# First conditioning split into two column halves, and the gate rows' transposes moved behind the second head's first blocks

## The chip, the cores and the metric

The kernel runs on one core of a Trainium2 chip. The metric is the device time of one execution in microseconds (us), the median of the runs shown. The engines are TensorE (PE in the profile; its weight loads are PEld), VectorE (DVE), ScalarE (ACT), GpSimd (POOL) and SyncE (SP), which issues nearly all DMAs.

## The reference, cut to what matters

The kernel is one inference step of a two-layer encoder on 1024 prompt tokens and 32 sample tokens, D = 1024, all in float32. Layer 0 is an mLSTM mixer with four heads. What concerns the change is the conditioning of its input and the value, gate and query/key projections of it:

```python
def ada_mod(c, w, b):
    return jax.nn.silu(c) @ w + b
...
sh1, sc1, g1, sh2, sc2, g2 = jnp.split(ada_mod(c, p['w_ada'][l], p['b_ada'][l])[:, None, :], 6, axis=-1)
u = x * (1 + sc1) + sh1
...
proj = u @ w_in
qk_pre = proj[..., :2 * QK_A]
v = proj[..., 2 * QK_A:2 * QK_A + V_A]
o_pre = proj[..., 2 * QK_A + V_A:2 * QK_A + 2 * V_A]
gates = (proj[..., 2 * QK_A + 2 * V_A:] + b_if).astype(jnp.float32)
qk, conv_new = causal_conv(qk_pre, conv_prev, conv_w, conv_b)
```

There is one vector c for the prompt and one for the sample. Before any u exists, sh1 and sc1 are needed: the first 2048 columns of a 1024 x 6144 weight, 8 MiB, that meet two vectors only.

## The kernel before

Tokens lie in three blocks, `TBS`: 384, 384 and 288 (256 prompt and the 32 sample tokens). Features lie on the partitions, in `KC` = 8 chunks of 128. Products run as three float32r matmuls each (high x high, high x low, low x high).

**The first conditioning.** `ada_load(k)` (L193) loads rows 128k to 128k + 127 of the first 2048 columns as two DMAs of 512 KB, each of 1024 columns, into a buffer of the ring tag "wc", which has six. `ada_mm(k)` (L424) multiplies them by the silu of c, one matmul of 512 columns for each of the four column groups of PE, and adds up over k in one PSUM bank. `ada_first` (L430) copies that to SBUF, transposes it and adds the bias: sh1 and sc1 for all eight chunks.

**The value stage.** `x_transpose` (L403) turns a block's rows of x into columns, chunk by chunk, on PE, and copies them out. `u_chunks` (L414) makes u of a chunk: high part on ACT (L370), the unrounded value and the low part on DVE (L372, L375). `v_weight` (L465) loads one half of the rows of head 0's value weights, to which the eight gate columns are added; `split` casts it on ACT (L89) and subtracts on DVE (L90). `v_first` (L504) runs over blocks and, in a block, over chunks outside and tiles of 128 tokens inside, three matmuls each (L479 to L481), so that a chunk can be used as soon as it is made. Behind each chunk it calls `next_u` (L759), which moves the next block's transposes and u along by one chunk.

**The gate rows.** `gate_rows` (L518) transposes the gate columns (L532), then makes the log-sigmoid, its running sums and maxima as rows of four partitions, on ACT and DVE, into a tile `stk`. After `yield GATE` comes its second part: nine transposes of `stk` (L567) and two copies into `ae`, which `mlstm` reads for its weights W (L654).

**The order.** The text is traced in order, and a scheduler places each instruction by its time model, with earlier text ahead where several could run; each engine then works through its own list in order. Side work stands in generators of a `Flow`: `tick` counts a waiting time down and runs the next piece. `qk_proj` (L571) makes a head's query and key: six blocks of 24 matmuls, the convolution on DVE (L596, L599) and the silu (L451 to L454, L604, L605); behind the first two blocks of each half and behind its end it calls `after`, which ticks. `GATE` = 3.0 lets the second part of `gate_rows` be traced at the third tick, in the middle of head 0's `qk_proj`; `flow.finish(gates)` behind it runs what is left. The scores of head 0 (`S`, L656) are the first work of `mlstm`, traced behind the third unit of head 1's `qk_proj`.

Of the kernel before, what the change touches and what calls it, by code (L numbers as in the profile page):

```python
# [8 lines left out]
F32 = mybir.dt.float32  # L9
F32R = mybir.dt.float32r  # L10
AF = mybir.ActivationFunctionType
ALU = mybir.AluOpType
# [63 lines left out]
def trunk_kernel(ctx: ExitStack, tc: tile.TileContext, a, o):  # L76
# [113 lines left out]
    def wc_tile(shape, name):  # L190
        return ring.tile(shape, F32, tag="wc", name=name, bufs=6)

    def ada_load(k):  # L193

        raw = wc_tile([P, 2 * D], f"rada_0_{k}")
        for i in range(2):
            nc.sync.dma_start(raw[:, i * D:(i + 1) * D], a["w_ada"][0, k * P:(k + 1) * P, i * D:(i + 1) * D])
        return raw
# [5 lines left out]
    nc.sync.dma_start(rows2[96:112], a["b_ada_kv"].rearrange("(k p) -> k p", p=P))  # L204
    adaw = [ada_load(k) for k in range(4)]
    tp = tpt("tp_c")
# [185 lines left out]
    def rc_tile(shape, name):  # L392
        return A.tile(shape, F32, tag="rc", name=name, bufs=1)
# [29 lines left out]

    def ada_mm(k):  # L424

        for q in range(4):
            nc.tensor.matmul(ada_ps[32 * q:32 * q + 32, :512], cs[:, k, :], adaw[k][:, q * 512:(q + 1) * 512],
                             start=(k == 0), stop=(k == KC - 1))

    def ada_first():  # L430

        sb = rc_tile([P, 512], "sada")
        ps2 = nmt("adat")
        for hf in range(2):
            (nc.scalar.copy if hf else nc.vector.tensor_copy)(sb[:, 256 * hf:256 * hf + 256],
                                                              ada_ps[:, 256 * hf:256 * hf + 256])
            for b in (2 * hf, 2 * hf + 1):
                nc.tensor.transpose(ps2[:, b * P:(b + 1) * P], sb[:, b * P:(b + 1) * P], ident)
        nc.vector.tensor_tensor(
            ada[:, 0:16, :].rearrange("p (q b) j -> p q b j", q=4),  # L440
            ps2.rearrange("p (b q j) -> p q b j", b=4, q=4)[:, :, :, 0:2],
            pt2[:, 0:16].rearrange("p (q b) -> p q b", q=4)[:, :, :, None].broadcast_to([P, 4, 4, 2]), op=ALU.add)


    GATE = 3.0
    ADA_C = (2.0, 0.0, 2.0)
# [292 lines left out]
    x_load(*TBS[0])  # L739
    adaw += [ada_load(k) for k in (4, 5)]  # L740
    for k in range(4):
        ada_mm(k)
    vw = [v_weight(0, 0)]
    adaw += [ada_load(k) for k in (6, 7)]
    for k in range(4, 6):
        ada_mm(k)
    for _ in xT[0]:
        pass
    for k in range(6, 8):
        ada_mm(k)  # L750
    vw.append(v_weight(0, 1))
    x_load(*TBS[1], wc_tile)
    x_load(*TBS[2])
    ada_first()
    for _ in uT[0]:
        pass
    flow.add(small_params(), SP)

    def next_u(bi, k):  # L759
        if bi < 2:  # L760
            next(xT[bi + 1])
            next(uT[bi + 1])
            if k == KC - 1:
                for g in (xT[bi + 1], uT[bi + 1]):
                    for _ in g:
                        pass
        flow.tick()
# [17 lines left out]
    qk = [qk_proj(0, tick)]  # L785
    flow.finish(gates)
    G = A.tile([P, KC, T], F32, tag="G", name="G")
    ml = None
    for h in range(1, NH):
        unit = [0]  # L790

        def after_qk():
            unit[0] += 1
            if h > 1 or unit[0] >= 3:
                flow.tick()
        if h == 1:
            ml = flow.add(mlstm(0, *qk[0], vts[0]))
        qk.append(qk_proj(h, after_qk))
        vts.append(v_proj(h, tick))
        flow.finish(ml)  # L800
        ml = flow.add(mlstm(h, *qk[h], vts[h]))
# [1289 lines left out]
```

## Time and profile before

| | us |
|---|---|
| median of 3 runs (lowest to highest) | 2438.1 (2436.41 to 2440.5) |
| profiled execution | 2437.59 |
| its span, first to last instruction | 2435.8 |
| PE busy in the span | 2363.6 (97%) |
| DVE busy | 1987.5 (82%) |
| ACT busy | 1178.8 (48%) |

The profile gives, for each engine, the time in which it worked, and for a wait the instruction that ended it. Times in a row are us from the span's start, then the duration; "x8" counts instructions, and what stands in brackets is the idle time ahead and who ended it. A PE that is busy is not always at its peak, since matmuls overlap.

### The profile page before, as it was taken

The numbers are of one execution on the slowest core, as the hardware profiler recorded it, in microseconds if no ns is written. First come the engines' busy times: TensorE is split into PE (matmuls) and PEld (weight loads), VectorE is DVE, ScalarE is ACT, GpSimd is POOL, SyncE is SP. The second block draws the span as 40 slices with busy tenths as digits, with TensorE's granted clock in tenths as the row PEclk, the third lists the DMA queues.
The fourth block names the chain that finished last, engine by engine and source line by source line (L and its number), as shares of the span: only waits on it lengthen the run. The fifth ranks groups of instructions, "written<-read, shape, count | busy, mean of one in ns | idle before, by whom it ended". The sixth has DMA issues, their size and how long they took to land.

```text
span 2435.8 us, 44452 instructions
## 1 busy us (share of the span) xinstructions
PE 2363.6 (97%) x17180; PEld 2265.8 (93%) x17180; DVE 1987.5 (82%) x4222; ACT 1178.8 (48%) x2394; POOL 166.6 (7%) x315
## 2 busy tenths in 40 slices
PE   7999999999999999999999999999999999899997
PEld 4999999999999999999989977889999999899997
DVE  4899898788788789999697666755998888887778
ACT  4644456278566620010157566763776777222212
POOL 0211100000000000000001134420000000000003
PEclk9999999999999999999999999999999999999999
DMA  8433223436556897656423220051486779966642
GB/s 297 128 103 98 82 86 102 158 113 215 182 186 194 296 343 266 234 203 232 143 64 97 74 64 1 11 133 36 162 279 233 252 255 341 367 242 232 229 151 72
DMA packets 292151, 423.61 MB, mean 174 GB/s; under 512 B 15576, under 2 KB 221804, under 8 KB 286820
## 3 DMA queue, kind: packets, MB, share of 16 engines
q1 hardware_dynamic: 287908, 390.50, 48.3%
q10 hardware_dynamic: 4032, 30.28, 3.1%
q8 instruction: 135, 2.21, 0.4%
q14 instruction: 76, 0.62, 0.1%
HBM read 304.91 MB, written 118.17 MB: 174 GB/s over the span
## 4 chain that ended last, share of the span: by engine, by line
PE 47%; DVE 12%; DMA 5%; ACT 4%; issue 2%; POOL 1%; SPq 0%; DVEq 0%; ACTq 0%; POOLq 0%
PE dn L1415 11%; PE up L1280 9%; PE dn L120 5%; PE dn L119 5%; PE dn L118 5%; PE pv L1853 3%; PE s L1796 2%; PE pt L1831 2%; DMA rdn_u<-in_w_up_dram 1%; DVE wf_u L90 1%; PE op_b L118 1%; PE op_b L119 1%; PE op_b L120 1%; DVE HL L90 1%; DMA radw<-in_w_ada_dram 1%
## 5 line engine op out<-in xcount | busy, mean ns | idle before, releaser
L1045 DVE SCALAR_TENSOR_TENSOR ACX<-dn,ada,ACX 128x264 f32<-128x264 f32 (+6 forms) x664 | 281.9, 448 | 86.4 <-PE dn L1415 41.4
L1415 PE MATMUL dn<-fx,wf_d 128*128 128x264 f32 x2016 | 254.0, 285 | 6.5 <-DVE ACX L1045 3.5
L1415 PEld LDWEIGHTS dn<-fx,wf_d 128*128 128x128 f32 x2016 | 248.7, 188 | 8.7 <-issue 2.5
L89 ACT CAST w_dn<-raw_dn 128x1024 fp32r<-128x1024 f32 x36 | 37.7, 1050 | 284.1 <-DVE aw L274 172.8
L118 PE MATMUL dn<-hs,w_dn 128*128 128x384 f32 (+2 forms) x512 | 161.3, 316 | 0.8 <-DVE ACX L1045 0.7
L119 PE MATMUL dn<-hs,w_dn 128*128 128x384 f32 (+2 forms) x512 | 160.9, 315 | 0.0
L120 PE MATMUL dn<-hs,w_dn 128*128 128x384 f32 (+2 forms) x512 | 155.9, 314 | 1.8 <-DVE w_dn L90 1.8
L1280 PE MATMUL up<-TF,wf_u 128*128 128x264 f32 x1056 | 143.6, 285 | 1.8 <-ACT H L1283 1.8
L1280 PE MATMUL up<-u,wf_u 128*128 128x264 f32 x1056 | 139.7, 285 | 1.7 <-DVE H L1286 0.8
L1280 PE MATMUL up<-U,wf_u 128*128 128x264 f32 x1056 | 139.6, 285 | 1.6 <-DVE H L1286 1.0
L274 DVE SCALAR_TENSOR_TENSOR aw<-radw,cs,aw 128x512 f32<-128x512 f32 x196 | 139.5, 745 | 0.0
L1280 PEld LDWEIGHTS up<-TF,wf_u 128*128 128x128 f32 x1056 | 134.3, 188 | 3.1 <-ACT H L1283 3.0
L1280 PEld LDWEIGHTS up<-U,wf_u 128*128 128x128 f32 x1056 | 133.1, 188 | 2.7 <-DVE H L1286 1.9
L1280 PEld LDWEIGHTS up<-u,wf_u 128*128 128x128 f32 x1056 | 132.6, 188 | 2.7 <-ACT wf_u L89 0.8
L119 PE MATMUL dn<-U,w_dn 128*128 128x384 f32 (+2 forms) x416 | 129.8, 313 | 0.0
L118 PE MATMUL dn<-U,w_dn 128*128 128x384 f32 (+2 forms) x416 | 129.3, 311 | 0.0
L120 PE MATMUL dn<-U,w_dn 128*128 128x384 f32 (+2 forms) x416 | 125.6, 312 | 0.9 <-DVE w_dn L90 0.9
L238 DVE SCALAR_TENSOR_TENSOR ada_room<-ada_room,cs 128x256 f32<-128x256 f32 x224 | 98.9, 476 | 4.2 <-DMA ada_room<-in_w_ada_dram 4.2
L120 PEld LDWEIGHTS dn<-hs,w_dn 128*128 128x128 f32 x512 | 95.8, 188 | 2.9 <-DVE w_dn L90 2.6
L118 PEld LDWEIGHTS dn<-hs,w_dn 128*128 128x128 f32 x512 | 96.4, 188 | 1.5 <-DVE ACX L1045 1.0
L119 PEld LDWEIGHTS dn<-hs,w_dn 128*128 128x128 f32 x512 | 96.5, 188 | 0.0
L1806 DVE CUSTOM_DVE_ANT_0 p<-s,bias 128x576 f32<-128x576 f32 (+9 forms) x132 | 79.1, 606 | 20.3 <-PE s L1796 13.4
(394 smaller groups left out, 7171.5 us busy)
## 6 DMA issues: line engine op xcount, KB each, us to landing
hpl<-HL SPq DMA_DIRECT2D x144, 264.0 KB
rdn_u<-in_w_up_dram SPq DMA_DIRECT2D x64, 512.0 KB
hd<-HL SPq DMA_DIRECT2D x28, 1056.0 KB
fx<-hd SPq DMA_DIRECT2D x50, 528.0 KB
radw<-in_w_ada_dram SPq DMA_DIRECT2D x24, 1024.0 KB
hd<-HM SPq DMA_DIRECT2D x28, 792.0 KB
raw_up<-in_w_up_dram SPq DMA_DIRECT2D x40, 512.0 KB
raw_dn<-in_w_down_dram SPq DMA_DIRECT2D x36, 512.0 KB
```

The source lines that it names most:

```text
L90: (eng or nc.vector).tensor_sub(dst_l, src, dst_h.bitcast(F32))
L118: nc.tensor.matmul(ps, wh, mov(0, k), start=(k == 0), stop=False)
L119: nc.tensor.matmul(ps, wh, mov(1, k), start=False, stop=False)
L120: nc.tensor.matmul(ps, wl, mov(0, k), start=False, stop=(k == nk - 1))
L238: nc.vector.scalar_tensor_tensor(acc[:, cnd], raw[:, k], sc, acc[:, cnd], op0=ALU.mult, op1=ALU.add)
L274: nc.vector.scalar_tensor_tensor(acc[cnd], raw[:, k], sc, acc[cnd], op0=ALU.mult, op1=ALU.add)
L1045: nc.vector.scalar_tensor_tensor(xs, ps[:, off + o:off + o + mm_], gate[:, fc, cnd:cnd + 1], xs, op0=ALU.mult, op1=ALU.add)
L1280: nc.tensor.matmul(p, self.ws[w][:, wl, k], moving(f, tp, xl, k), start=first and k + n_ == 0, stop=k == 3 and n_ == 2, skip_group_check=n ...
L1415: nc.tensor.matmul(p, ws[w][:, wl, k], t[:, s0, xl], start=first and k + n_ == 0, stop=k == kg - 1 and n_ == 2, skip_group_check=not first)
L1796: nc.tensor.matmul(s[:, b, :w], qst, kk[i][:, g, k0 + j0:k0 + j0 + w], start=(i == 0), stop=(i == 1))
L1806: nc.vector.tensor_tensor_reduce(out=z.rearrange("p (b w) -> p b w", b=np_), in0=s[:, :np_, :w], in1=bt.rearrange("p (b w) -> p b w", b=np ...
L1853: nc.tensor.matmul(pv[64 * e:64 * e + 64, :nq], V[:kp, vt0 + j, g * 64:(g + 1) * 64], pts[e][:kp, j, :nq], start=(j == 0), stop=(j == nt - 1))
```

## The change

The first conditioning is loaded and multiplied by halves. Half `hf` holds 512 of the 1024 columns of sh1 and the same 512 of sc1: all that four of the eight chunks need. Half 0 is loaded first, ahead of block 0's rows; half 1 behind the first value weights. `ada_first(0)` is traced ahead of the x transposes, the first four chunks of u of block 0 follow, and `v_first` starts on them; behind its fourth chunk come half 1's products, `ada_first(1)`, block 0's last four chunks of u, and the small parameters. Block 1's transposes and u move along by two chunks for each of the last four chunks instead of by one for each of eight. `GATE` becomes 99.0, so that no tick reaches the second part of `gate_rows`, and `flow.finish(gates)` moves into head 1's `qk_proj`, behind its second block; the tile `G` is taken there too.

```diff
--- before.py
+++ after.py
@@ -190,11 +190,13 @@
     def wc_tile(shape, name):
         return ring.tile(shape, F32, tag="wc", name=name, bufs=6)
 
-    def ada_load(k):
-
-        raw = wc_tile([P, 2 * D], f"rada_0_{k}")
+    def ada_load(hf, j):
+
+        raw = wc_tile([P, 2, 2, 512], f"rada_0_{hf}_{j}")
         for i in range(2):
-            nc.sync.dma_start(raw[:, i * D:(i + 1) * D], a["w_ada"][0, k * P:(k + 1) * P, i * D:(i + 1) * D])
+            k = 2 * j + i
+            nc.sync.dma_start(raw[:, i], a["w_ada"][0, k * P:(k + 1) * P, :2 * D].rearrange(
+                "p (r h c) -> p h r c", r=2, h=2)[:, hf])
         return raw
     c_rows = raw_tile([16, P], "c_rows")
     nc.sync.dma_start(c_rows[0:8], a["c_prompt"].rearrange("b (k p) -> (b k) p", p=P))
@@ -202,7 +204,7 @@
     rows2 = raw_tile([NPT2, P], "rows2")
     nc.sync.dma_start(rows2[0:96], a["b_ada"].rearrange("l (k p) -> (l k) p", p=P))
     nc.sync.dma_start(rows2[96:112], a["b_ada_kv"].rearrange("(k p) -> k p", p=P))
-    adaw = [ada_load(k) for k in range(4)]
+    adaw = [[ada_load(0, j) for j in range(4)]]
     tp = tpt("tp_c")
     nc.tensor.transpose(tp[:, :16], c_rows, ident[:16, :16])
     cx = cp.tile([P, 4, 16], F32, name="cx")
@@ -421,28 +423,30 @@
 
     ada_ps = adat("ada_0")
 
-    def ada_mm(k):
+    def ada_mm(hf, k):
 
         for q in range(4):
-            nc.tensor.matmul(ada_ps[32 * q:32 * q + 32, :512], cs[:, k, :], adaw[k][:, q * 512:(q + 1) * 512],
+            nc.tensor.matmul(ada_ps[32 * q:32 * q + 32, 256 * hf:256 * hf + 256], cs[:, k, :],
+                             adaw[hf][k // 2][:, k % 2, q // 2, q % 2 * 256:q % 2 * 256 + 256],
                              start=(k == 0), stop=(k == KC - 1))
 
-    def ada_first():
-
-        sb = rc_tile([P, 512], "sada")
-        ps2 = nmt("adat")
-        for hf in range(2):
-            (nc.scalar.copy if hf else nc.vector.tensor_copy)(sb[:, 256 * hf:256 * hf + 256],
-                                                              ada_ps[:, 256 * hf:256 * hf + 256])
-            for b in (2 * hf, 2 * hf + 1):
-                nc.tensor.transpose(ps2[:, b * P:(b + 1) * P], sb[:, b * P:(b + 1) * P], ident)
-        nc.vector.tensor_tensor(
-            ada[:, 0:16, :].rearrange("p (q b) j -> p q b j", q=4),
-            ps2.rearrange("p (b q j) -> p q b j", b=4, q=4)[:, :, :, 0:2],
-            pt2[:, 0:16].rearrange("p (q b) -> p q b", q=4)[:, :, :, None].broadcast_to([P, 4, 4, 2]), op=ALU.add)
-
-
-    GATE = 3.0
+    def ada_first(hf):
+
+        sb = rc_tile([P, 256], f"sada{hf}") if hf else y_tile([P, 256], "sada0")
+        ps2 = nmt(f"adat{hf}")
+        for b in range(2):
+            cols = slice(b * P, (b + 1) * P)
+            (nc.scalar.copy if b else nc.vector.tensor_copy)(sb[:, cols], ada_ps[:, 256 * hf + b * P:256 * hf + b * P + P])
+            nc.tensor.transpose(ps2[:, cols], sb[:, cols], ident)
+        for r in range(2):
+            c0 = r * KC + 4 * hf
+            nc.vector.tensor_tensor(
+                ada[:, c0:c0 + 4, :].rearrange("p (q b) j -> p q b j", q=2),
+                ps2[:, :256].rearrange("p (b r q j) -> p r q b j", b=2, r=2, q=2)[:, r, :, :, 0:2],
+                pt2[:, c0:c0 + 4].rearrange("p (q b) -> p q b", q=2)[:, :, :, None].broadcast_to([P, 2, 2, 2]), op=ALU.add)
+
+
+    GATE = 99.0
     ADA_C = (2.0, 0.0, 2.0)
     w_in = a["w_in_a"][0]
 
@@ -737,33 +741,40 @@
     xT = [x_transpose(t0, n, (nc.scalar.copy, nc.vector.tensor_copy)[:2 - (i > 0)]) for i, (t0, n) in enumerate(TBS)]
     uT = [u_chunks(t0, n) for t0, n in TBS]
     x_load(*TBS[0])
-    adaw += [ada_load(k) for k in (4, 5)]
-    for k in range(4):
-        ada_mm(k)
+    for k in range(KC):
+        ada_mm(0, k)
     vw = [v_weight(0, 0)]
-    adaw += [ada_load(k) for k in (6, 7)]
-    for k in range(4, 6):
-        ada_mm(k)
+    adaw.append([ada_load(1, j) for j in range(4)])
+    ada_first(0)
     for _ in xT[0]:
         pass
-    for k in range(6, 8):
-        ada_mm(k)
     vw.append(v_weight(0, 1))
     x_load(*TBS[1], wc_tile)
     x_load(*TBS[2])
-    ada_first()
-    for _ in uT[0]:
-        pass
-    flow.add(small_params(), SP)
+    for k in range(4):
+        next(uT[0])
 
     def next_u(bi, k):
-        if bi < 2:
-            next(xT[bi + 1])
-            next(uT[bi + 1])
-            if k == KC - 1:
-                for g in (xT[bi + 1], uT[bi + 1]):
-                    for _ in g:
-                        pass
+        if bi == 0:
+            if k == 3:
+                for i in range(KC):
+                    ada_mm(1, i)
+                ada_first(1)
+                for _ in uT[0]:
+                    pass
+                flow.add(small_params(), SP)
+            if k < 4:
+                return
+            for _ in range(2):
+                next(xT[1])
+                next(uT[1])
+        elif bi == 1:
+            next(xT[2])
+            next(uT[2])
+        if bi < 2 and k == KC - 1:
+            for g in (xT[bi + 1], uT[bi + 1]):
+                for _ in g:
+                    pass
         flow.tick()
     vts = [v_first(vw, next_u)]
     for t0, n in TBS:
@@ -783,14 +794,16 @@
         ada_fix(0, [(2, "g"), (4, "sc"), (5, "g")])
     flow.add(ada_l0())
     qk = [qk_proj(0, tick)]
-    flow.finish(gates)
-    G = A.tile([P, KC, T], F32, tag="G", name="G")
     ml = None
     for h in range(1, NH):
         unit = [0]
 
         def after_qk():
+            nonlocal G
             unit[0] += 1
+            if h == 1 and unit[0] == 2:
+                flow.finish(gates)
+                G = A.tile([P, KC, T], F32, tag="G", name="G")
             if h > 1 or unit[0] >= 3:
                 flow.tick()
         if h == 1:
```

## The prediction

> **What bounds the kernel now.** I read the page first, then the stretches of the first 200 us, because all edits lie there.
>
> ```profile
> span 2435.8 us, 44452 instructions
> ...
> PE 2363.6 (97%) x17180; PEld 2265.8 (93%) x17180; DVE 1987.5 (82%) x4222; ACT 1178.8 (48%) x2394; POOL 166.6 (7%) x315
> ```
>
> TensorE (PE) is busy 97% of the span. The 72.2 us in which it is not are therefore the place to look for a gain, and time taken out of PE's own stream ahead of a full stretch should shift everything behind it. In the stretches the columns are: length, busy us and instructions of PE, of its weight loads (PEld), DVE, ACT and POOL, then the granted clock, the DMA share and GB/s.
>
> ```profile
> 16.60:20.20 3.60, 1.45 (x7) 0.74 (x8) 0.56 (x1) 0.48 (x1) 0.00 (x0) 1.00 1.03 421
> 20.20:25.00 4.80, 4.80 (x20) 1.98 (x20) 1.12 (x3) 0.96 (x2) 0.00 (x0) 0.64 1.04 385
> ...
> 29.00:34.00 5.00, 4.21 (x16) 0.58 (x16) 1.26 (x1) 0.04 (x1) 0.00 (x0) 1.00 1.03 411
> 34.00:36.45 2.45, 1.06 (x7) 0.62 (x7) 1.44 (x5) 1.13 (x3) 0.00 (x0) 1.00 1.03 410
> 36.45:70.80 34.35, 34.35 (x265) 32.15 (x266) 26.51 (x78) 25.80 (x57) 1.33 (x7) 1.00 0.73 224
> 70.80:92.70 21.90, 21.85 (x134) 21.19 (x131) 19.62 (x32) 10.93 (x18) 1.90 (x2) 1.00 0.49 142
> 92.70:94.90 2.20, 0.02 (x1) 0.00 (x0) 2.20 (x5) 1.38 (x2) 0.06 (x2) 1.00 0.04 8
> 94.90:99.60 4.70, 4.65 (x28) 4.60 (x29) 4.61 (x8) 2.86 (x4) 0.77 (x2) 0.64 0.09 33
> 99.60:140.00 40.40, 40.36 (x270) 39.34 (x270) 39.62 (x89) 29.91 (x80) 11.29 (x22) 1.00 0.20 64
> 140.00:200.00 60.00, 58.15 (x381) 53.37 (x380) 55.49 (x184) 26.53 (x80) 8.02 (x24) 1.00 0.35 104
> ```
>
> Three stages show. Until 36.45 us the DMA engines are the bound: their share is 1.03 and PE does conditioning products as rows land. From 36.45 to 70.80, the value work of the first head, PE is busy without a gap and DVE has 7.8 us to spare. At 92.70 PE stops for 2.20 us and then runs 4.70 us at a granted clock of 0.64. From there to 140 us DVE (39.62 of 40.40) is as full as PE. Who waits for whom, PE's weight loads, 36 to 140 us:
>
> ```profile
> PEld ae_ps L567 <- ACT stk L560: 2.5, 1, 2.5
> ...
> PEld S L656 <- DVE y L605: 0.4, 1, 0.4
> ```
>
> So the stop is the wait of the gate rows' transposes (L567). The second row matters as much: head 0's first score product S(0) already arrives 0.4 us too early for DVE.
>
> **Part 1: conditioning by halves.** The rows of the opening, in order of time:
>
> ```profile
> 26.03 1.07 PE L427 MATMUL ada<-rada,cs 128*32 128x512 f32 x8
> ...
> 27.97 1.07 ACT L89 CAST w_v<-raw_v 128x1056 fp32r<-128x1056 f32 x1 [0.65 <-DMA raw_v<-in_w_in_a_dram]
> 29.07 1.26 DVE L90 TENSOR_TENSOR w_v<-raw_v,w_v 128x1056 fp32r<-128x1056 f32 x1 [0.47 <-ACT w_v L89]
> ...
> 32.94 1.05 PE L427 MATMUL ada<-rada,cs 128*32 128x512 f32 x4 [0.23 <-DMA rada<-in_w_ada_dram]
> ...
> 34.04 0.42 DVE L435 COPY sada<-ada 128x256 f32<-128x256 f32 x1 [3.71 <-PE ada L427]
> 34.50 0.37 ACT L435 COPY sada<-ada 128x256 f32<-128x256 f32 x1 [5.46 <-DVE sada L435]
> ...
> 36.45 0.39 PE L479 MATMUL v<-w_v,U 128*128 128x264 f32 x1 [0.86 <-ACT U L370]
> ```
>
> Before, the last conditioning rows land at 32.94 us and the first value product starts at 36.45. After, half 0 is 4.2 MB of the 8.4, so chunks 0 to 3 need 4.2 MB plus block 0's rows (1.6 MB) and the first value weights (0.5 MB) instead of 11.0 MB. At the 400 GB/s of the window below that is 4.7 MB, 11.8 us, fewer: the data is there near 21 us. Cast and subtraction of the weights (1.07 + 1.26) put the first products near 24 us, and their 36 matmuls end before 30 us, under the cover of half 1's transfer.
>
> Chunk 4 needs all 11.0 MB still: either half 1 or the second value weights come last, in an order that I can't tell. If half 1 is last, it lands at 32.94 plus what shorter rows cost. A row of a half is 2 KB where it was 4 KB. Two windows with only such rows, 1124 to 1126 us (2 KB, radw) and 7 to 15 us (nearly all 4 KB):
>
> ```profile
> DMA packets 389, 0.80 MB, mean 398 GB/s; under 512 B 0, under 2 KB 0, under 8 KB 389
> ```
> ```profile
> DMA packets 880, 3.20 MB, mean 400 GB/s; under 512 B 99, under 2 KB 99, under 8 KB 880
> ```
>
> 398 against 400 GB/s is 0.1 us on 8.4 MB, so half 1 lands near 33.1 us. The Trainium skill's "DMA: Bandwidth & Descriptors", "Why small descriptors are slow (HBM only)", speaks against the change here: about 3 cycles of overhead a packet beside one per 32 bytes. By it two 2 KB packets take 134 cycles for the 131 of one of 4 KB, and an estimate from that page is 0.5 us on the opening instead of 0.1. The trace's two windows agree with a small loss and not with a large one.
>
> From the last landing to chunk 4: before, 36.45 - 32.94 = 3.51 us. The last product is half as wide (0.5 us less than 1.05), the two copies half as wide (about 0.1 less each), two transposes fewer (0.2), one small DVE add more (0.15, an estimate from the copies): 2.8 us, so 35.9. If the weights are last, 33.1 + 1.07 + 1.26 and two handovers give 35.6. I take 36.0: 0.45 us before the old start. Bounds: 35.6, and 36.8 if the steps run at a low clock.
>
> What is gained beside that is the work of chunks 0 to 3. In the stretch from 36.45 to 70.80 PE's stream is the bound, as these two rows show (a stretch of value products alone, and the x transposes of the whole stage):
>
> ```profile
> 64.00:70.00 6.00, 6.00 (x52) 6.00 (x51) 2.36 (x2) 1.65 (x2) 1.04 (x3) 1.00 1.03 304
> ```
> ```profile
> L410 PE MATMUL xps<-ident,xr 128*128 128x128 f32 (+1 forms) x46 | 8.3, 271 | 0.0
> ```
>
> A product comes each 6.00 / 50 = 0.12 us (two of the 52 are cut by the edges). 9 tiles x 8 chunks x 3 = 216 products make 25.9 us and the transposes 8.3: 34.2 of 34.35. Block 0's first four chunks are 3 x 4 x 3 = 36 products, 4.3 us, that now run in the wait. The stage ends 4.3 + 0.45 = 4.75 us earlier. The rest of it stays covered: DVE and ACT have 7.8 and 8.5 us to spare there and also lose four chunks of it; block 1's rows come behind the same 11.0 MB; its buffers come free as half 1's products run, as before.
>
> Against this stands PE's clock. Between the first half's end and chunk 4 PE does one product per 1.3 us. All four column groups of 512 took 1.07 us together (26.03), so 256 take 0.54: busy 41%. The nearest row, 16.60 to 20.20, is busy 1.45 / 3.60 = 40%, and behind it the clock is 0.64 for 4.80 us, 1.7 us lost; but a product at half clock is busy 0.8 of the time, like 29.00 to 34.00 (0.84, clock 1.00), so the clock may be back before chunk 4. Cost 0 to 1.7 us; I take 0.4, nearer to that last row. Part 1 in sum: 4.75 - 0.4 = 4.35 us gained, bounds 2.3 and 5.2. The small parameters move behind half 1's products, in SP's queue too; the first reader is the gate rows' bias, behind 70.80 us, so I cost that at nothing. Were they late, the gate chain would be, on the same DVE path as below.
>
> **Part 2: the gate rows' transposes.** The rows are of the gate chain's start, its end, and of S(0):
>
> ```profile
> 70.80 1.03 PE L532 MATMUL gt<-ident,g 128*36 128x128 f32 x8
> ...
> 92.42 0.30 PE L120 MATMUL qk<-U,w_qk 128*128 128x288 f32 x1
> ...
> 93.81 1.08 ACT L560 ACTIVATE stk<-tt 4x1056 f32<-4x1056 f32 x1 [0.37 <-DVE tt L559]
> ...
> 94.95 0.72 PE L567 MATMUL ae_ps<-ident,stk 36*128 36x36 f32 x9 [2.23 <-ACT stk L560]
> ```
> ```profile
> 113.56 0.95 DVE L605 SCALAR_TENSOR_TENSOR y<-y,sl 128x353 f32<-128x353 f32 x2
> ...
> 114.13 0.30 PEld L656 LDWEIGHTS S<-y,y 128*128 128x128 f32 x2 [0.36 <-DVE y L605]
> ```
>
> Stop 94.95 - 92.42 - 0.13 = 2.4 us, low clock 4.70 x 0.36 = 1.7 us: 4.1 us in all. Moved past two blocks of the second head (48 products of some 0.175, 8.4 us), plus what is left of head 0's projection, the transposes come far behind the chain's end, 24 us after its start. The stop at L567 goes for certain. What is late next is S(0): PE would reach it 4.1 us earlier, while its y comes from DVE:
>
> ```profile
> 77.80:113.50 35.70, 34.76 (x52) 0.95 0.24 74
> ```
> ```profile
> DVE y L596 <- ACT qkp L588: 0.7, 1, 0.7
> ```
>
> From 77.80 on DVE has 0.94 us of idle time in 35.70 (columns: length, DVE busy, clock, DMA), 0.7 of it a wait that PE's earlier end removes. The change takes no work off DVE there. So S(0) can come at most 0.9 us earlier and PE stops there for 4.1 + 0.4 - 0.9 = 3.6 us; if that again costs a low clock, 1.7 us go once more. Part 2: between -0.8 (0.9 - 1.7) and +4.1 (if the schedule places S(0) later among PE's products). I take +0.35, near DVE's idle time.
>
> **Sum.** 4.35 + 0.35 = 4.7 us off the profiled execution, whose own time is 2437.6 (its span 2435.8 and 1.8 around it): 2432.9. The median of the runs is 2438.1, 0.5 more: 2433.4. No wait on PE behind 200 us has to do with either part, so I carry the shift to the end unchanged. 0.2%, 4.9 us, is about what a measurement of this kernel can tell from no change; the bound lies at 2433.2.
>
> **Rivals.** (a) Both stops go: S(0) stands later in PE's order, or DVE's later gaps (4.5 us from 140 to 200) repay it. For it: PE had no longer wait than 0.4 us there. Against it: 34.76 of 35.70. 4.35 + 4.1 gives 2429.7.
>
> (b) The change doesn't do what it says: the schedule puts half 1's products ahead of the first chunks' values on PE. Then values start once the last product ends, 33.1 + 0.6 = 33.7, and chunk 4 is ready when they are through: 36.45 - 33.7 = 2.75 gained, 2435.0 with part 2.
>
> (c) Slower: the clock closes again and again behind S(0). From 99.60 to 140 PE is now paced by DVE, and each stop like that of 92.70 costs 1.7 us of low clock behind it. From six such stops on, 10.2 us, the 4.7 are gone and 4.9 more: 2443 to 2446. For it: 20.20 and 94.90 both show the drop after a thin stretch. Against it: no second stop over 0.4 us in these rows. The Trainium skill's "TensorE: Matmul & The Clock Gate", "Part 1: The HAM clock gate", has the clock at half after a window of about 3.4 us without enough work; by that page one stop costs at most half of such a window, 1.7 us, which the trace bears out (1.7).
>
> **Chances.** Forecast 0.47, (a) 0.24, (b) 0.15, (c) 0.14. The forecast lies on the bound: its own range is 2431 to 2437 and somewhat under half of it is faster than 2433.2. Faster 0.22 + 0.24 = 0.46; same 0.25 + 0.13 = 0.38; slower 0.14 and 0.02 of (b) = 0.16. The range reaches from (a) with its bound, 2428.5, to 2442, just short of (c).
>
> **What would show it.** Value products (L479 to L481 now) begin near 24 us, stop before 30, and go on near 36; the gate transposes of head 0 (L532) start near 66 instead of 70.80; PE has no wait at the ae_ps transposes; a wait of 2 to 4 us on y by S(0) appears near 109 us, and DVE is over 97% busy before it. The prediction is wrong if chunk 4 starts after 37 us, if S(0) doesn't wait, or if the clock from 100 to 140 us falls under 0.95.

## The result, and the profile after

| | before | after |
|---|---|---|
| median (lowest to highest), 22 runs each | 2438.63 (2433.29 to 2441.81) | 2444.76 (2438.64 to 2449.91) |
| profiled execution | 2437.59 | 2447.85 |

The ratio after to before is 1.0028, interval [1.0021, 1.0034]: 6 us slower where 4.7 us less was forecast. One execution of the changed kernel can differ from another by 11 us, and the profiled one lies 3 us over the median, so its 10 us of loss show the places better than the sizes. A second profile of the same kernel (below, `after_again`) is 4 us shorter.

The page of the changed kernel, its span and the busy time of each engine:

```profile
span 2445.7 us, 44589 instructions
...
PE 2367.0 (97%) x17244; PEld 2274.0 (93%) x17244; DVE 1989.8 (81%) x4226; ACT 1179.6 (48%) x2395; POOL 167.1 (7%) x315
```

PE's busy time grew by 3.4 us; the other 6.5 us of the longer span are new idle time. The changed kernel's rows of the opening on PE, with start, duration, instruction and the idle time ahead of it:

```profile
24.24 0.96 PE L483 MATMUL v<-w_v,U 128*128 128x264 f32 x3
...
34.91 0.64 PE L429 MATMUL ada<-rada,cs 128*32 128x256 f32 x8 [0.71 <-DMA rada<-in_w_ada_dram]
...
37.72 0.39 PE L483 MATMUL v<-w_v,U 128*128 128x264 f32 x1 [0.91 <-ACT U L372]
...
67.75 0.81 PE L536 MATMUL gt<-ident,g 128*36 128x128 f32 x6
```

Values start at 24.24 us, the last rows of half 1 land at 34.91, chunk 4 starts at 37.72, and the gate transposes come at 67.75 instead of 70.80: the halves give 3.05 us there in this execution. It is the best of twelve. In the twelve profiles of kernels with the halves (those of the experiments below among them), whose text is the same up to there, chunk 4 starts at 37.68 to 38.81 us and the gate transposes at 67.75 to 70.34, median 69.2; in the seven with the old loads these come at 70.77 to 71.99, median 70.9. 1.7 us is the typical gain.

The changed kernel's stretches (length, busy us of PE, PEld, DVE, ACT, POOL, then granted clock, DMA share, GB/s):

```profile
29.00:34.00 5.00, 4.59 (x68) 2.82 (x66) 0.41 (x1) 0.00 (x0) 0.00 (x0) 1.00 1.05 389
...
78.00:113.00 35.00, 32.56 (x206) 31.69 (x204) 34.83 (x53) 18.09 (x39) 10.19 (x13) 1.00 0.30 91
113.00:120.00 7.00, 6.92 (x32) 6.81 (x33) 6.77 (x12) 3.81 (x12) 0.87 (x4) 0.76 0.01 2
...
140.00:200.00 60.00, 56.09 (x371) 51.62 (x369) 53.94 (x178) 25.53 (x75) 9.69 (x23) 1.00 0.39 113
420.00:470.00 50.00, 46.85 (x277) 46.05 (x277) 40.80 (x90) 13.14 (x24) 0.00 (x0) 0.97 0.71 234
```

From 78 to 113 us DVE is full (34.83 of 35). Then PE loses time at several places where it lost none or less: in 140 to 200 it does 56.09 us of work (58.15 before), and in 420 to 470 it has 3.15 us of idle time and a clock of 0.97 (before, 50.00 of 50.00 at 1.00). Who PE waits for from 60 to 480 us (total us, times, longest), in the changed kernel and in the kernel before:

```profile
PE cu L682 <- DVE hn L708: 5.8, 5, 1.9
PE op_a L118 <- ACT w_oa L89: 3.1, 1, 3.1
PE S L660 <- DVE y L609: 2.4, 1, 2.4
```
```profile
PE ae_ps L567 <- ACT stk L560: 2.2, 1, 2.2
PE cu L678 <- DVE hn L704: 2.0, 5, 0.9
```

The stop at ae_ps is gone and one at S(0) has come, as forecast. But the head's value updates (`cu`) wait 3.8 us more for DVE, and 436.50 us has a stop that nobody spoke of: the first products of the output projection (`op_a`) wait for a cast of its weights (`w_oa`). By the first rows of named operations in the two traces the changed kernel is 3.0 us ahead at the gate transposes, 1.0 ahead at S(0), 3.3 behind at head 0's state (`co`, 170), 5.2 behind at the first `op_a` (419), 10.7 behind at the next stage (`mean_n`, 466), and 9.9 at the end. The loss is made between 113 and 470 us. Behind that the order of instructions on PE and DVE is the same in both kernels.

### The profile page after: what moved, and what is told of

Its sections match the earlier page's. It is cut to its first block, busy times and chain, and to the rows that moved or that the text cites. A ratio compares the mean times of both kernels' runs of the same rounds, so it can differ in the third digit from the quotient of the medians.

```text
span 2445.7 us, 44589 instructions
## 1 busy us (share of the span) xinstructions
PE 2367.0 (97%) x17244; PEld 2274.0 (93%) x17244; DVE 1989.8 (81%) x4226; ACT 1179.6 (48%) x2395; POOL 167.1 (7%) x315
## 4 chain that ended last, share of the span: by engine, by line
PE 51%; DVE 10%; ACT 4%; DMA 2%; issue 2%; POOL 1%; SPq 0%; DVEq 0%; ACTq 0%; POOLq 0%
PE dn L1428 12%; PE up L1293 10%; PE dn L120 5%; PE dn L119 5%; PE dn L118 5%; PE pv L1866 3%; PE s L1809 2%; PE pt L1844 2%; DMA rdn_u<-in_w_up_dram 1%; PE op_b L118 1%; PE op_b L120 1%; PE op_b L119 1%; PE q L119 1%; PE q L120 1%; PE q L118 1%
```

## The experiments

Each is compared with runs of the kernel before on the same chip. "Halves alone" is part 1 alone.

**1. One part at a time.** `p1_only` is the changed kernel with `GATE` and `flow.finish(gates)` put back; `p2_only` is the kernel before with only these moved; `gate_end` has one number changed; `s_late` is the changed kernel with head 0's scores traced two units later.

```diff
 p1_only, against the changed kernel          p2_only is the reverse, in the kernel before
-    GATE = 99.0
+    GATE = 3.0
+    flow.finish(gates)      # behind qk = [qk_proj(0, tick)], and no longer in after_qk
 gate_end, against the kernel before
-    GATE = 3.0
+    GATE = 99.0
 s_late, against the changed kernel
-            if h > 1 or unit[0] >= 3:
+            if h > 1 or unit[0] >= 5:
```

> Part 1 alone: conditioning by halves as changed, the gate rows' transposes where they were before (GATE 3.0, finish(gates) right behind head 0's projection). Theory A (the loss comes from part 2: its stop moves to S(0), costs the clock there, and the mlstm stage never recovers): value stage ends 3 us earlier as in the changed kernel, the stop at the ae_ps transposes is there as before, and the kernel is 3 us faster than before (ratio 0.9985 to 0.999). Theory B (part 1 shifts the scheduler's times, and the new order of DVE's and PE's work in the mlstm stage from 113 to 470 us costs some 10 us whatever the gate transposes do): slower than before by 4 to 8 us, with PE waits on hn and on w_oa as in the changed kernel.

> Part 2 alone: gate rows' transposes behind head 1's second block, conditioning as before. Theory A: no stop at ae_ps, a stop of 2 to 4 us at S(0) on DVE's y with a low clock behind it, and a kernel that is 2 to 8 us slower than before. Theory B: the stop moves to S(0), but the order behind it is nearly that of before, so the sum is within 2 us of before.

> Before, with GATE 99.0 alone: finish(gates) stays right behind head 0's projection, so that the nine transposes move back by about 20 products (2.7 us) instead of 70. Both theories: the 2.2 us stop at ae_ps goes or falls under 0.5 us; if DVE is the bound to 140 us, S(0) waits 2 to 3.5 us for y instead and the time is within 2 us of before; if PE's stop was a real loss, 3 to 4 us faster.

> The changed kernel with head 0's first scores traced two units later (head 1: ticks from unit 5 on instead of 3). Theory A: S(0) stands later among PE's products, its stop and the low clock behind it are gone, and the kernel is 3 to 5 us faster than the changed one (about 2440). Theory B: the order of the rest decides, S(0)'s stop goes but other waits stay, and the time lies within 2 us of the changed kernel's or anywhere the new order puts it.

| | median (runs) | ratio to before |
|---|---|---|
| p1_only | 2447.35 (11) | 1.0038 [1.0027, 1.0049] |
| p2_only | 2439.10 (11) | 1.0003 [0.9995, 1.0012] |
| gate_end | 2437.95 (12) | 1.0000 [0.9990, 1.0009] |
| s_late | 2445.71 (10) | 1.0034 [1.0023, 1.0044] |

The longest waits of PE in `gate_end`, then in `p1_only`:

```profile
PE S L656 <- DVE y L605: 2.5, 1, 2.5
```
```profile
PE cu L682 <- DVE hn L708: 4.6, 5, 2.8
PE op_a L118 <- ACT w_oa L89: 2.9, 1, 2.9
PE ae_ps L571 <- ACT stk L564: 2.1, 1, 2.1
```

Part 2 does what the prediction said and is worth nothing: the stop of 2.2 us at ae_ps becomes one of 2.5 at S(0). `s_late` took the wait at S(0) away, and PE waited elsewhere. All of the loss is in part 1 (the intervals of `p1_only` and of the whole change overlap), although its value stage ends earlier (gate transposes at 69.0 us). It has the same stop at `op_a`.

**2. The order behind the value stage.** From `flow.finish()` behind `v_first` to the end of the output gates' projection, the halves alone trace the same 3775 instructions, one for one, as the kernel before. The scheduler, working by its own time model, still lists them in another order on each engine: of DVE's 958 positions 903 hold another instruction. So the order can be exchanged. The ties below fix only in which order an engine takes its instructions; the list of pairs comes from the other kernel's built program.

```diff
+    def pin(n0):                      # n0: instructions traced up to the value stage's end
+        got = traced[n0:]
+        for seq in order:             # one list for each engine
+            for i, j in zip(seq, seq[1:]):
+                tc.add_manual_dep(got[j], got[i].name, order only)
```

> The halves alone (part 1), with the 3775 instructions traced behind the value stage, up to the end of the output gates' projection, tied on every engine to the order in which the kernel before has them (order-only ties, no work and no wait added). Theory B1, the loss of the halves is the other order of that stretch: with the old order back, the 3 us that the value stage ends earlier stay, about 2434 us, 3 below the kernel before. Rival B2, the loss comes from the halves themselves (2 KB rows, another place of the transfers, other buffers), whatever the order: it stays near the halves alone, 2447.

> The kernel before, with the same stretch tied on every engine to the order that the kernel with the halves alone has. No half, no 2 KB row, the value stage as before. Theory B1 (order): 10 to 13 us slower than the kernel before, 2448 to 2450, with the wait of PE on the output projection's weights (w_oa) near 430 us. Rival B2 (the halves themselves): as the kernel before, 2437 to 2438.

| | median (runs) | ratio to before |
|---|---|---|
| before_pinp: before, order of the halves | 2448.34 (5) | 1.0040 [1.0026, 1.0054] |
| p1_pinb: halves, order of before | 2440.99 (11) | 1.0012 [1.0003, 1.0020] |

PE's waits in `before_pinp`:

```profile
PE cu L786 <- DVE hn L812: 4.6, 6, 2.8
PE op_a L226 <- ACT w_oa L197: 3.6, 1, 3.6
```

This is the main finding. The kernel before, with nothing changed but the order of what comes behind its value stage, loses as much as the halves alone, at the same two places. With the old order back, the halves lose 3 us instead of 10. B2 falls as the main cause; B1 holds for the order, but its second half (3 us kept) fails.

**3. Which stretch of the order.** The same ties on a part of the instructions: `p1_h1b` and `before_h1p` from head 1's query and key on, `p1_qk0b` all but the gate rows, `after_tailb` and `before_tailp` from the output gates' projection on.

```diff
-            for i, j in zip(seq, seq[1:]):
+            for i, j in pairs(seq, both traced from the named place on):
```

> The halves alone; what is traced behind the first part of the gate rows, from the conditioning's side work and head 0's query and key on, is tied to the order of the kernel before. The gate rows are free, so that ACT reads the gate columns ahead of the next cast of weights, which the full tie had behind it (PE waited 2.5 + 1.2 us for them at 71 to 76 us). Theory B1 (the loss of the halves is the order behind the value stage): the head start of 3 us is kept, 2434 to 2436, below the kernel before. Rival B3 (an earlier end of the value stage is worth nothing, since VectorE bounds the stretch from 78 to 113 us and takes the gain): 2437 to 2439.

> The halves alone; only what is traced from head 1's query and key on is tied to the order of the kernel before; gate rows and head 0's query and key stay in the scheduler's order for the halves. If the loss is made behind head 0 (about 120 to 470 us): 2434 to 2439. If it is made in head 0's stretch, 70 to 115 us, where the side work's first piece comes 15 us later: 2443 to 2447.

> The kernel before; only what is traced from head 1's query and key on is tied to the order that the halves alone have there. If the loss is made behind head 0: 2446 to 2448, with the wait of PE on the output projection's weights near 430 us. If it is made in head 0's stretch: 2438 to 2440.

> The changed kernel; only what is traced from the output gates' projection on (behind about 310 us, to 470 us) is tied to the order that the kernel before has there. Theory: half of the loss is the stop of 3.1 us at the output projection's weights at 436.5 us with its low clock, because the conditioning's pieces stand ahead of the last splits of u on VectorE: 5.4 us better than the changed kernel, 2439 to 2440, and no wait on w_oa over 1 us. Rival: the side work is late there because it was late all along, and the tie only moves the stop: 2443 to 2446.

> The kernel before; only what is traced from the output gates' projection on is tied to the order that the halves alone have there. Theory: the stop at the output projection's weights comes, 5 us slower than before, 2443. Rival: without late side work there is no stop, 2438 to 2439.

| | median (runs) | ratio to before |
|---|---|---|
| before_tailp | 2444.64 (11) | 1.0027 [1.0018, 1.0036] |
| before_h1p | 2443.49 (6) | 1.0032 [1.0020, 1.0043] |
| after_tailb | 2444.41 (11) | 1.0027 [1.0017, 1.0038] |
| p1_h1b | 2444.08 (5) | 1.0038 [1.0025, 1.0050] |
| p1_qk0b | 2442.90 (7) | 1.0032 [1.0021, 1.0044] |

The kernel before had a median of 2438.60 beside the two tail runs and of 2435.08 beside the other three. The tail's order alone costs it 6 us. `before_h1p`, with the halves' order from head 1 on, loses 7.8 us and has both stops (`cu` 2.9 us, `op_a` 3.1), so most of the 10 us of `before_pinp` lie behind head 0. Why the tail costs so much, the rows of ACT and DVE show, first in the changed kernel, then in the kernel before:

```profile
435.41 2.00 ACT L89 CAST w_oa<-raw_oa 128x1024 fp32r<-128x1024 f32 x2 [6.24 <-DVE U L90]
```
```profile
431.65 0.62 DVE L243 TENSOR_SCALAR ada_room<-ada_room,cs 128x256 f32<-128x256 f32 x2 [0.28 <-DMA ada_room<-in_w_ada_dram]
432.18 2.46 DVE L240 SCALAR_TENSOR_TENSOR ada_room<-ada_room,cs 128x256 f32<-128x256 f32 x6
434.55 0.82 DVE L90 TENSOR_TENSOR U<-G,U 128x288 fp32r<-128x288 f32 x2
...
435.68 1.22 DVE L90 TENSOR_TENSOR w_oa<-raw_oa,w_oa 128x1024 fp32r<-128x1024 f32 x1
```
```profile
422.53 2.46 DVE L238 SCALAR_TENSOR_TENSOR ada_room<-ada_room,cs 128x256 f32<-128x256 f32 x6
424.91 1.56 DVE L90 TENSOR_TENSOR U<-G,U 128x288 fp32r<-128x288 f32 x4
426.50 2.00 ACT L89 CAST w_oa<-raw_oa 128x1024 fp32r<-128x1024 f32 x2 [3.68 <-DVE U L90]
```

In both kernels the cast of the weights waits for DVE's last splits of u (L90), and a piece of the conditioning's side work (`ada_l0`) stands directly ahead of these in DVE's list. What differs is how much of it does. By the rows between the first product of `op_a` and the last split, DVE does 13 instructions of side work there before, 5.5 us, and 18 in the changed kernel, 7.6 us, with a wait of 0.28 us for a load. All six profiles with the halves' order in the tail that were counted have 18 to 20, all seven with the old one 13. The splits come at 434.55 and the cast 8.9 us later than before, 5.2 of which the changed kernel is behind already; 2.1 of the other 3.7 are this side work. PE goes on at 436.50. The profile of `before_tailp` has that stop (3.0 us), those of both runs of `after_tailb` do not (PE 49.96 of 50.00 in 420 to 470).

The other way round the result is not clean. `after_tailb`'s median stands where the changed kernel's does, though both its profiled executions (2440.26 and, in a repeat called `after_tailb2`, 2442.27) lie below it, and at `mean_n` they are 4.3 and 6.1 us behind the kernel before, where the changed kernel is 10.7 and 9.0 in two profiles; where its other executions lose the time is open. And ties on a part make the scheduler order the rest anew: `p1_qk0b` got a wait of 6.4 us at S(0), `p1_h1b` one of 3.6 at `cu` (2.8 in the halves alone), and both are as slow as the halves alone within their intervals. So the tail's price is shown by `before_tailp`; how the rest is spread is not.

**4. Where the 3 us of the halves go.** `p1_pinb2` is `p1_pinb` with ACT reading the gate columns ahead of the second cast of query/key weights (in `p1_pinb` PE stood 2.5 and 1.2 us for them). `after_pinb2` is the whole change, tied on every engine to the order of `p2_only`, with the same repair. The `noside` pair leaves out multiply-adds of the side work (14 of the 16 for a pair of column blocks; the expectation miscounts).

```diff
 p1_pinb2 and after_pinb2, ACT's list (PE's gate transposes likewise)
-  vt_8, cast w_qk, cast w_qk, gate columns (six reads), cast w_qk
+  vt_8, gate columns (two), cast w_qk, gate columns (four), cast w_qk, cast w_qk
 noside, in ada_cols
-                for k in range(4):
+                for k in range(4 if base != 16 else 1 - half):
```

> The halves alone with the order of the kernel before behind the value stage, as in the full tie, but ACT reads the gate columns ahead of the second cast of weights and PE transposes them as the halves alone do; VectorE's and SyncE's order stays that of before. It takes away the 2.5 + 1.2 us that PE stood at the gate transposes in the full tie. Theory B1 (the earlier end of the value stage is kept where the order behind it suits): 2435 to 2438, that is 1 to 3 below the kernel before on the same chip. Rival B3 (VectorE bounds the stretch from 78 to 113 us, and the head start is worth nothing there): as the full tie or at best as before, 0 to +3.

> The kernel before without 15 of the 16 multiply-adds of each half and pair of columns of layer 0's other conditioning (the side work on VectorE; its loads, transposes and sums stay): about 15 x 16 x 2 x 0.4 us / 2 of VectorE's work gone. It is the partner of the next run; by itself 0 to 6 us faster than the kernel before, since its order is planned anew.

> The changed kernel with the same multiply-adds left out. Theory C1, VectorE's full stretch and the place of the side work take the head start of the halves: against the partner the difference turns from +6 to between -3 and 0. Theory C2, the halves cost something of their own behind the value stage: it stays at +3 to +10 against the partner.

> Both parts of the change, with the order that the kernel before has when only its gate rows are moved (p2_only, 2439) tied on every engine behind the value stage; ACT reads the gate columns ahead of the second cast of weights. No side work comes late, no stop at the gate rows' transposes, no stop at the output projection's weights. If part of the head start can be kept: 2435 to 2437, 1 to 3 below the kernel before. If VectorE takes it all: PE stops 4 to 6 us at the scores of head 0 and the time is 2438 to 2441.

> The changed kernel, profiled a second time. What is the same in every execution by the first profile: the stop at head 0's scores (2.4 us), the late side work, the stop of 3 us at the output projection's weights; S(0) near 113, mean_n 8 to 11 us later than in the kernel before. What may differ is the low clock behind the stops, some us in all.

| | median (runs) | ratio to before |
|---|---|---|
| p1_pinb2 | 2441.55 (11) | 1.0010 [1.0001, 1.0019] |
| before_noside | 2440.33 (11) | 1.0013 [1.0005, 1.0022] |
| after_noside | 2441.29 (12) | 1.0022 [1.0013, 1.0031] |
| after_pinb2 | 2439.00 (11) | 1.0003 [0.9994, 1.0012] |
| after_again | 2443.71 (1) | |

`after_pinb2` settles the sum as far as it can be measured: both parts of the change, in the order of `p2_only` with the repair, take 0.7 us more than the kernel before (1.5 less to 2.9 more by the interval) instead of 6. Most or all of the loss is order, and no gain of the change can be seen. It doesn't beat the kernel before, nor does any other kernel here. `p1_pinb2` lost both stops at the gate columns and is no faster than `p1_pinb`: in its profile PE waits 5.8 us at ae_ps instead. That is B3's time, not B1's. Without the side work's arithmetic the change costs 1.0 us against its partner by the medians and 2.2 by the ratios instead of 6, between C1's range and C2's; both kernels of that pair are slower than the kernel before with all its work, probably by a newly planned order, which was not tested. `after_again`, the changed kernel once more, has the stops of the first profile: 2.3 us at S(0), 2.7 at `op_a`, 9.0 us behind at `mean_n`.

Two lists suggest why nothing is gained, SyncE's and ACT's. SyncE's issues from 42 us on (start, us until the last of the group), in the kernel before and in the changed one:

```profile
42.72 9.36 SPq L770 DMA_DIRECT2D xsp<-xt  x2
52.18 6.14 SPq L96 DMA_DIRECT2D raw_qk<-in_w_in_a_dram  x5
62.44 0.52 SPq L770 DMA_DIRECT2D xsp<-xt  x1
63.05 0.62 SPq L231 DMA_DIRECT2D ada_room<-in_w_ada_dram  x1
```
```profile
43.19 16.71 SPq L781 DMA_DIRECT2D xsp<-xt  x3
60.00 10.19 SPq L96 DMA_DIRECT2D raw_qk<-in_w_in_a_dram  x7
70.24 0.50 SPq L233 DMA_DIRECT2D ada_room<-in_w_ada_dram  x1
```

Each block's x columns are stored (`xsp`) behind its transposes. Before, two stores stood ahead of the query/key weights; now the third does too, waits for block 2's columns until 59 us, and the weights' loads start at 60.00 instead of 52.18, the side work's first at 70.24 instead of 63.05. DVE, which needs both, is then short of work. But ACT's list has changed too. In the kernel before, then in the changed one:

```profile
63.64 2.01 ACT L89 CAST w_qk<-raw_qk 128x1024 fp32r<-128x1024 f32 x2
70.26 1.10 ACT L486 COPY vt<-v 128x256 f32<-128x256 f32 x3 [4.62 <-PE v L481]
```
```profile
67.21 0.38 ACT L490 COPY vt<-v 128x256 f32<-128x256 f32 x1 [5.45 <-PE v L485]
67.48 1.05 ACT L89 CAST w_qk<-raw_qk 128x1024 fp32r<-128x1024 f32 x1
```

Before, ACT casts the first two query/key weights ahead of the copies of the last value tiles; now one of these copies stands ahead of the first cast and waits for PE. The semaphore updates in the traces have the first cast's two loads landed at 60.11 us before and at 67.25 in the changed kernel, so there the load and the copy let the cast go at nearly the same time. From 60 to 80 us, DVE's busy time is the third figure with a count, in the kernel before, the changed one and `after_pinb2`:

```profile
60.00:80.00 20.00, 19.95 (x141) 19.20 (x140) 13.16 (x34) 14.93 (x28) 1.04 (x3) 1.00 0.84 241
```
```profile
60.00:80.00 20.00, 19.36 (x134) 18.49 (x134) 9.94 (x24) 14.39 (x25) 1.04 (x3) 1.00 0.88 245
```
```profile
60.00:80.00 20.00, 19.29 (x133) 18.11 (x132) 10.13 (x24) 14.28 (x26) 1.04 (x3) 1.00 0.90 250
```

DVE does 3.2 and 3.0 us less in these 20 us. By 60 us it had done 2.1 and 1.6 us more, so at 80 us it is 1.1 and 1.4 us behind (40.62 and 40.30 us of work since the start against 41.70). From 78 to 113 us it is the busiest engine (34.83 of 35 in the changed kernel, 33.12 in `after_pinb2`): PE's head start is one that DVE has lost. In `after_pinb2` PE then stands 3.4 us at 97.95 for ACT's copies, which have DVE's gate rows ahead of them, and S(0) starts 0.5 us ahead of before. The stores and these copies are traced ahead of the tied stretch, so no tie moved them against the weights: in all 12 profiles with the halves the query/key loads start at 60.0 to 62.6 us, in the eight without them at 52.1 to 54.2. That the late weights cost the head start is read from these rows. Whether the store holds them back or ACT's list is not shown: a kernel with the third store behind the weights was not run, and with ACT's list as it is it might gain nothing.

**5. The shorter rows.** `before_2k` cuts the rows of the first conditioning in the kernel before, and nothing else:

```diff
-            nc.sync.dma_start(raw[:, i * D:(i + 1) * D], a["w_ada"][0, k * P:(k + 1) * P, i * D:(i + 1) * D])
+            nc.sync.dma_start(raw.rearrange("p (r h c) -> p r h c", r=2, h=2)[:, :, i],
+                              a["w_ada"][0, k * P:(k + 1) * P, :2 * D].rearrange("p (r h c) -> p r h c", r=2, h=2)[:, :, i])
```

> The kernel before; each pair of loads of the first conditioning is cut into rows of 2 KB (512 of shift, 512 of scale) instead of 4 KB, in the same order and to the same places. If the shorter rows make the 1.35 us for each 512 KB, the last of the 16 lands 0.9 to 1.1 us later than 32.94 us and the first value product starts near 37.5 us instead of 36.5. If it was the order of the loads (all of half 1 at the end), both stay.

> The changed kernel with the order of before from the output gates' projection on, a second time, for its profile. If the first profile was typical: no wait on w_oa, and the loss between the first output-projection product and the end of that stage under 1 us (5.4 us in the changed kernel); what differs in its time from the first profile then lies in the stops of 110 to 310 us.

The stretch of `before_2k` in which the last of these rows land, and its first value product:

```profile
29.00:34.00 5.00, 3.14 (x9) 0.51 (x10) 2.45 (x2) 1.07 (x1) 0.00 (x0) 0.73 1.05 390
```
```profile
38.45 0.39 PE L481 MATMUL v<-w_v,U 128*128 128x264 f32 x1 [0.87 <-ACT U L372]
```

390 GB/s as in the changed kernel (389), against 411 with rows of 4 KB: the row's length, not the order of the halves, takes 5% (from 5 to 33 us 378 and 382 GB/s against 395, 4%). Values start 2.0 us later than in the profile of the kernel before, where 1 us was expected; a clock of 0.73 stands beside it, and the first value products of the seven kernels with rows of 4 KB start at 36.39 to 37.63 us. PE, DVE and ACT take their instructions in the order of the kernel before. Of the 2.0 us 1.3 are left at S(0) and 1.0 at the first `op_a`, but nothing at 863 us (`dn`), and its one time, 2437.83, is 0.7 us over the median beside it. So even in an unchanged order a shift of the opening comes through in part at most.

## Why the prediction was wrong

**Part 1's gain at its own place: right in kind, too large.** Taken 4.35 with bounds of 2.3 and 5.2; the gate transposes came 3.05 us earlier in the profiled execution and 1.7 in the median of twelve, under the lower bound. Two terms were mis-sized. The first is the landing of half 1: 33.1 taken, 34.91 measured. From there chunk 4 took 2.81 us, as forecast (2.8), and so started at 37.72, where 36.0 was taken and 36.8 was the upper bound, past the 37 us that were named as a sign of error. The landing was forecast from two windows at 398 and 400 GB/s. Both were full (DMA share 1.03 and 1.02), but they did not compare the two rows in one place; in 29 to 34 us rows of 2 KB ran at 389 and rows of 4 KB at 411, which on 8.4 MB is 1.2 us instead of 0.1. The other 0.6 us are open. The Trainium skill's "DMA: Bandwidth & Descriptors", "Why small descriptors are slow (HBM only)", which the prediction set aside at 0.5 us by an estimate, had the right direction; the trace shows more than twice its size. The second term is the clock, 0.4 us taken. It stayed at 1.00 in the profiled execution, but in seven of the twelve it fell to 0.5 for some us behind the wait for chunk 4; from chunk 4 to the gate transposes these took 31.3 to 31.6 us and the other five 30.0.

**Part 2: right.** PE has no wait at ae_ps over 0.3 us, waits 2.4 us for y at S(0) (3.6 taken, 2 to 4 named) after a stretch in which DVE is busy 34.83 of 35, and the clock behind that stop is 0.76 for 7 us, 1.7 us lost, as priced. Behind the same stop it stays at 1.00 in `after_again` and `gate_end`, so that price is not due each time; nor is it the most that one stop can cost, as the prediction has it: behind stops of 2.24 and 2.27 us at ae_ps in `before_tailp` and `before_h1p` the clock was 0.51 and 0.52 for 7 us, 3.4 us lost. `p2_only` at 1.0003, with an interval of 1.2 us less to 2.9 more, agrees with the forecast's "+0.35": no gain that can be measured.

**"So I carry the shift to the end unchanged": the step that failed.** It supposed that behind the edits the instructions stay in their places and only move in time. The edits changed the scheduler's time picture, and it listed DVE, PE, ACT and SyncE anew for 400 us. `before_pinp` prices that at 10.3 us for the halves' order; `after_pinb2`, 0.7 us over the kernel before instead of 6, puts most or all of the changed kernel's loss to it. The sentence ahead of it, that no wait behind 200 us has to do with either part, was argued from what the edits touch; the stop at 436.50 shows it wrong. And `before_2k` suggests that in an unchanged order, too, little of a shift reaches the end.

**What is late next: half seen.** The prediction named DVE as the next bound for part 2 but let part 1's 4.35 us through it, although it showed DVE with 0.94 us of idle time in 35.70; S(0) came 1.0 us earlier, at 113.08, where 109 was named. And it sent the small parameters through SP's queue but did not ask where the stores of x would stand in it.

**Rival (a)** did not come: the stop at S(0) is there. **Rival (c)** has nearly the measured time (2443 to 2446) by another mechanism: from 99.60 to 140 us there is one closing of the clock, behind S(0), not six. **Rival (b)** looked for a changed order in the wrong stretch: half 1's products did not get in front of the first values, since chunks 0 to 3 ran from 24.24 on.

## What to carry to other kernels

Where a scheduler lists the instructions, an edit at the start can change the order of everything behind it, and that can cost more than the edit saves; compare the built lists of the two kernels first, and tie the old order to the new kernel (and the new order to the old kernel) to tell the edit from its order. A gain on one engine lasts only if the next bound gets its inputs earlier too: follow the loads of the engine that is full behind the edit through their queue. And since a kernel whose engines wait for each other varies from execution to execution (11 us here, 8.5 before), one profile shows where time can be lost, several show where it is lost each time, and the median gives the size.

## What the runs showed of the hardware that was not expected

Rows of 2 KB in a full stretch of loads landed at 389 and 390 GB/s where rows of 4 KB landed at 411 (29 to 34 us; 408 to 410 in the other six profiles with rows of 4 KB). `before_2k` is the kernel before but for these rows.

A stop of PE of 2 to 3 us does not always cost clock. The 20 profiles have 30 stops of 2.0 to 3.6 us between 40 and 480 us. In the 7 us behind 23 of them the granted clock was lower, mostly 0.76 or 0.77 (1.7 us lost) and down to 0.51; behind seven it was 1.00. One kernel shows both at the same place. Behind the stop at `op_a`, 3.15 us in the changed kernel's first profile and 2.71 in its second (the figure ahead of the DMA share is the clock):

```profile
437.00:444.00 7.00, 7.00 (x33) 7.00 (x32) 7.00 (x14) 0.40 (x1) 0.00 (x0) 0.76 1.06 373
```
```profile
437.00:444.00 7.00, 7.00 (x41) 7.00 (x40) 7.00 (x14) 0.24 (x1) 0.00 (x0) 1.00 1.05 371
```

Between the first `op_a` and `mean_n`, the rows around that stop, the first lost 10.7 - 5.2 = 5.5 us to the kernel before and the second 3.5. The five profiles with that stop and a lower clock behind it lost 5.2 to 6.0 us for 2.9 to 3.6 us of waiting, the two without the lower clock 3.5 and 3.6 for 2.7. So a stop costs about 1.3 times its wait there, and about 1.7 to 1.8 times where the clock falls.
